# A hybrid mLSTM and window-attention decoder step on one core: all eight K tiles of the output product as seven products of sums of blocks

## The chip, the core and the metric

The kernel runs on one core of one Trainium2 chip. The metric is the device time of one execution in microseconds (us). TensorE is called PE here, its weight loads PEld, VectorE DVE, ScalarE ACT, GpSimd POOL and SyncE SP; SP issues most of the DMAs and is a queue in order like the others.

## The reference, cut to what matters

One layer of a decoder, for 1024 prompt rows and 32 sample rows (8 sequences of 4), all in float32 with D_MODEL = 1024:

```python
(mq, mk, mv, mi, mf, mo, mz, aq, ak, av, az, gm, ga) = split_in(h @ w_in)
y_m, C, n, m = mlstm_branch(mq, mk, mv, mi, mf, mo, mz, C0, n0, m0, b_i, b_f, g_mn)
...
y_a = o.astype(x.dtype) * jax.nn.silu(az)
u = jax.nn.sigmoid(gm) * (y_m @ w_mo) + jax.nn.sigmoid(ga) * (y_a @ w_ao)
x = x + gate * (u @ w_o)
```

followed by a final RMSNorm of x. The last product, u @ w_o (1024 + 32 rows, 1024 x 1024 weights), is the output product that this change is about. The gate is multiplied into the weights beforehand.

## The kernel before

A float32 product on PE is made of three products of rounded parts: each operand is split into a high part (a copy by ACT that rounds) and a low part (a subtract on DVE, the operand less its high part), and PE adds high by high, high by low and low by high. Such a split of a tile of 128x512 is one ACT copy and one DVE subtract; the names are wh_/wl_ for weights, h and l at the end of other names.

The program runs through these stages on PE: inputs and conditions; the "jobs" of queries and heads; eighteen "pairs" (class Pair, run by block_products), which form the gates and the remaining input products; the products of the attention output (att_products); eight jobs of w_m_out (mem_out, tile names g_w_mo, 288 matmuls of 384 or 288 columns); the output product in four blocks of 256 rows (class Rows; accumulators foX, foZ, foW, foY); and a short tail of norms and stores.

Pairs, attention output and part of the output product use the scheme of seven products for 2 x 2 blocks (Strassen in Winograd's form): four blocks of the one operand and four of the other become seven sums each, named 1 to 7, and seven products of half the K and half the columns take the place of eight. On the side of the weights the seven are b11, b21, b22, t1, t2, t3 and t4 (the table OPERANDS). [...]

Before the change the output product was mixed. K tiles 0 to 3 went through the seven products: two K tiles by three parts, six matmuls of 128x512 for each product, 42 for a block of 256 rows. K tiles 4 to 7 went plainly: 4 tiles by 3 parts by 4 accumulators, 48 matmuls. A block of rows had 90.

What sets the order of the work: PE's instructions run in the order in which the program writes them (in_order). In the middle part of the program DVE and ACT aren't tied to that order (V.on = S.on = False from L1935): the scheduler of the language orders them by its own estimates, and a multiplication written under not_before may not move ahead of the instruction written before it. From the row stage on (L2214) they are in written order again. Once built, every engine takes its instructions strictly in its own order. The class Side runs side work as generators in streams beside the pairs: each yield gives the time after which the next step may be written. Three of them matter here:

- stream "g", out_weights (L1964): started at pair 5, product 6. It loads w_out in tiles of 128x512 (wor), multiplies them by the gate (gb), forms the sums for K tiles 0 to 3 (wost, wos) and stores 22 tiles of float32 in DRAM (woD).
- the samples' heads, sample_head(h) (L1179): a chain of small operations on DVE, ACT and PE for the 32 sample rows. For h = 1 and h = 3 it ends with the tile sz being scaled on DVE (two small TENSOR_SCALAR), transposed on PE into sty (two matmuls at L280), and read by gs on DVE. fsden, fsv, fsr_w and fsr_y are the small steps of its reciprocal roots.
- the last four pairs are head_gate (names phead_gate): hg1z, hg, gts and zt are their evacuations on DVE, wr_mo, wr_mz and ws their raw weights and sums, and bx, bz, bw, by their accumulators.

In the stage of the w_m_out jobs the 22 stored tiles were loaded back into raw tiles and split there: high parts on ACT, low parts (wo_..l) on DVE and POOL in turns. A job of w_m_out has three pieces of columns (384, 384, 288); each piece is evacuated by a SCALAR_TENSOR_TENSOR (tgw_mo) and an add into u (u_h, u_l), on POOL for the last two jobs. The weights of a job, wr_w_mo, are split into wh_w_mo and wl_w_mo ahead of it; the third matmul of a job is the first that reads wl_w_mo.

Of the kernel before, what the change touches and what calls it, by code (L numbers as in the profile page):

```python
# [20 lines left out]
D = 1024  # L21
# [152 lines left out]
def body(tc, a):  # L174
    nc = tc.nc
    with ExitStack() as ctx:
# [1429 lines left out]
        u = lambda k, c0, n: ut[k // 4][:, k % 4, c0:c0 + n]  # L1606
# [36 lines left out]
        class AttPair:  # L1643
# [28 lines left out]
            def samples_end(self):  # L1672
                o = pb([128, 64], "smpo")
                mm(o, self.sums, cst[:, C_S64:C_S64 + 64], start=True, stop=True)
                us = ut[self.i // 2][:, 2 * self.i % 4:2 * self.i % 4 + 2, SEQ:T]
                V.scalar_tensor_tensor(us, self.ts, 1.0, o.rearrange("p (c s) -> p c s", c=2), op0=ALU.add, op1=ALU.mult)
# [287 lines left out]
        def out_weights():  # L1964
# [5 lines left out]
            def keep(name, k, t):  # L1970
                woD[name, k] = dp.tile([128, 512], F32, name=f"woD{name}{k}")
                store(woD[name, k], t)

            def load(ks):
                raws = {}
                for k in ks:
                    for f in range(2):
                        raws[k, f] = ht([128, 512], f"wor{k}{f}")
                        dma(raws[k, f], a["w_out"][k * 128:(k + 1) * 128, HALF[f]])
                return raws  # L1980

            def summed(n, k, x, y, op):
                t = ht([128, 512], f"wos{n}{k}")
                V.tensor_tensor(t, x, y, op=op)
                keep(n, k, t)
                return t

            lots = (4,), (5,), (6,), (7,), (0, 2), (1, 3)
            ahead = [load(lots[0])]
            yield 5.0, ""  # L1990
            for i, ks in enumerate(lots):
                raws = ahead.pop()
                if i + 1 < len(lots):
                    ahead.append(load(lots[i + 1]))
                yield 3.0, ""
                for (k, f), t in raws.items():
                    with not_before(V):
                        V.tensor_tensor(t, t, gb[f], op=ALU.mult)
                    if len(ks) == 1:
                        keep(f"p{f}", k, t)  # L2000
                    elif (k, f) != (ks[0], 1):
                        keep(("b11", "", "b21", "b22")[2 * (k // 2) + f], ks[0], t)
                    yield 2.4, ""
                if len(ks) == 2:
                    k = ks[0]
                    b11, b12, b21, b22 = raws.values()
                    t3 = summed("t3", k, b22, b12, ALU.subtract)
                    yield 2.4, ""
                    summed("t1", k, b12, b11, ALU.subtract)
                    yield 2.4, ""  # L2010
                    t2 = summed("t2", k, b11, t3, ALU.add)
                    yield 2.4, ""
                    summed("t4", k, b21, t2, ALU.subtract)
                    yield 2.4, ""

# [39 lines left out]
        class Rows:  # L2055


            def __init__(self, i):
                self.i, self.w, self.g = i, {}, {}
                self.x = [[t[:, :, (2 * i + c) * 128:(2 * i + c + 1) * 128] for t in ut] for c in range(2)]  # L2060

            def split(self, n, src, home, o):
                if home not in self.g:
                    self.g[home] = [ht([128, 4, 128], f"u{t}{home}", F32R) if home == "E" else
                                    granule(f"u{self.i}{t}{home}", t, 4, F32R) for t in ("wh", "wl")]
                hi, lo = (t[:, o:o + src.shape[1]] for t in self.g[home])
                S.copy(hi, src)
                V.tensor_tensor(lo, src, hi.bitcast(F32), op=ALU.subtract)
                self.w[n] = hi, lo

            def start(self, *ns):
                (a1, p1), (a2, p2) = self.x
                for n in ns:
                    if n == 1:
                        self.s = blocks_of_rows[self.i - 1].x[1][0][:, 2:4] if self.i else at["qpad"].rearrange("p b k g t -> p (b k g t)").rearrange("p (c e) -> p c e", e=128)
                        self.split(1, a1[:, 0:2], "A", 0)
                        V.tensor_tensor(self.s, a2[:, 0:2], a2[:, 2:4], op=ALU.add)
                    elif n == 5:
                        self.split(5, self.s, "A", 2)
                        V.tensor_tensor(a2[:, 0:2], a1[:, 0:2], a2[:, 0:2], op=ALU.subtract)  # L2080
                        V.tensor_tensor(a1[:, 0:2], self.s, a1[:, 0:2], op=ALU.subtract)
                    elif n == 2:
                        self.split(2, a1[:, 2:4], "B", 0)
                        V.tensor_tensor(a1[:, 2:4], a1[:, 2:4], a1[:, 0:2], op=ALU.subtract)
                    else:
                        self.split(n, *{6: (a1[:, 0:2], "B", 2), "p1": (p1, "C", 0), "p2": (p2, "D", 0), 7: (a2[:, 0:2], "E", 2),
                                        3: (a1[:, 2:4], "E", 0), 4: (a2[:, 2:4], "F", 0)}[n])

            def product(self, n, o, first, c0=0, w=512):
                hi, lo = self.w[n]  # L2090
                for k in range(2):
# [3 lines left out]
                    mm(o, lo[:, k], bh, start=False, stop=(k == 1), more=not first)  # L2095

            def plain(self, c, th, o, ks=range(4), c0=0, w=512):
                hi, lo = self.w[f"p{c + 1}"]
                for k in ks:
                    bh, bl = (t[:, c0:c0 + w] for t in plain[4 + k, th])  # L2100
                    mm(o, hi[:, k], bh, start=False, stop=False, more=True)
                    mm(o, hi[:, k], bl, start=False, stop=False, more=True)
                    mm(o, lo[:, k], bh, start=False, stop=(k == ks[-1]), more=True)

        blocks_of_rows = [Rows(i) for i in range(4)]
        wo, plain = {n: {} for n in ("b11", "b21", "b22", "t1", "t2", "t3", "t4")}, {}
        parts = [(n, k) for k in range(2) for n in ("b11", "t1", "b21", "t2", "b22", "t3", "t4")] + [(f"p{f}", k) for k in range(4, KT) for f in range(2)]
        side.finish("g")
        for d in range(KT):
            if d == KT - 1:  # L2110
                blocks_of_rows[0].start(1, 5, 2, 6)
            mem_out(d, ymx, u)
            for j in range(min(22, d * 26 // KT), min(22, (d + 1) * 26 // KT)):
                n, k = parts[j]
                raw = raw_tile(f"wo{n}{k}").rearrange("p k n -> p (k n)")
                dma(raw, woD[n, k], True)
                hi = ht([128, 512], f"wo_{n}h", F32R)
                lo = ht([128, 512], f"wo_{n}l", F32R) if j < 15 else granule(f"wo_{n}l", "wr", 9, F32R).rearrange("p k n -> p (k n)")
                S.copy(hi, raw)
                (G if j % 2 else V).tensor_tensor(lo, raw, hi.bitcast(F32), op=ALU.subtract)  # L2120
                if n[0] == "p":
                    plain[k, int(n[1])] = hi, lo
                else:
                    wo[n][k] = hi, lo

# [14 lines left out]
        def add_row(xb, c, src, kept=None):  # L2140
            if kept is not None:
                V.tensor_tensor(kept, kept, src, op=ALU.add)
            V.tensor_tensor(xb[:, c], xb[:, c], src if kept is None else kept, op=ALU.add)
# [25 lines left out]
        def sample_rows():  # L2169
# [14 lines left out]
            for f in range(2):  # L2184
# [4 lines left out]
                sums.append(raw_tile("fo8s").rearrange("p k n -> p (k n)")[:NS])  # L2189
# [16 lines left out]
        def copied(src, name, pool=None, c=slice(0, 512), new=None):  # L2206
            t = ht([128, 512], name) if pool is None else pool([128, 512], name)[:, :c.stop - c.start]
            if new:
                mm(t, new.w[1][0][:, 0], wo["b11"][0][0][:, c], start=True, stop=True)
# [7 lines left out]
        blocks_of_rows[0].start("p1")  # L2217
        xb = ss = None
        for i, r in enumerate(blocks_of_rows):
            nxt = blocks_of_rows[i + 1] if i < 3 else None  # L2220
# [3 lines left out]
            X, Z = pg([128, 512], "foX"), pa([128, 512], "foZ")  # L2224
            r.product(1, X, True)
            W = copied(X, "foW", pg, new=r if i == 0 else None)
            if i:
                add_row(before[0][1], lo, Y[0])
            r.product(5, Z, True)
            p5 = copied(Z, "fop5")  # L2230
            r.start("p2", 7, 3)
# [8 lines left out]
            if not nxt:  # L2240
                for c in range(2):
                    rows_out(4 + c, before[0][c], rs[:, c:c + 1])
            r.product(2, X, False)
            r.plain(0, 0, X)
# [139 lines left out]
```

## Time and profile before

| | us |
|---|---|
| median of 3 runs | 830.18 |
| range of the runs | 829.81 to 830.42 |
| the profiled execution | 829.68 |
| its span | 827.9 |
| PE busy | 810.2 |
| DVE busy | 590.5 |
| ACT busy | 419.0 |
| POOL busy | 67.2 |

A row of the page's group view names the line, the engine, the operation, the tile written and the tiles read, the shape, and then the busy time, the mean of one and the idle time ahead of it. In the timeline a row begins with start and duration in us, and ends, where the engine idled before it, with the idle time and what released it. A matmul's duration includes its drain, so that its pitch, from one start to the next, is shorter than its duration. A row of the windows view gives a stretch, its length, and for each engine its busy time and (x) its instructions, then the clock that PE was granted as a share of full speed, the DMA engines' busy share and GB/s.

### The profile page before, as it was taken

Reading aid. Unit: us, or ns where it says so; the run is one execution under the profiler, and the core shown is the slowest. Engines: PE = TensorE matmul, PEld = TensorE weight load, DVE = VectorE, ACT = ScalarE, POOL = GpSimd, SP = SyncE. Lnnn points to the kernel's source line nnn. Section 1 sums busy time; section 2 is a strip of 40 time slices with the busy share of each in tenths; the row PEclk is TensorE's granted clock in tenths of the full one; section 3 lists DMA queues with packets and bytes.
Section 4 is the critical chain, followed back from the end, with each engine's and each line's share of the span. In section 5 each row is a group of like instructions: output and inputs, shape, how many; then the busy total and the mean of one; then the engine's idle time right before and its main releaser. Section 6 shows DMA issues by size and latency. Waiting matters only on the chain.

```text
span 827.9 us, 15032 instructions
## 1 busy us (share of the span) xinstructions
PE 810.2 (98%) x5129; PEld 670.4 (81%) x5129; DVE 590.5 (71%) x1479; ACT 419.0 (51%) x1030; POOL 67.2 (8%) x128
## 2 busy tenths in 40 slices
PE   6999999999999999999999999999999999999996
PEld 3779897888787888888888878888888789987775
DVE  4899886746646456475667886897669988864776
ACT  5664365556455564545455454544446654344343
POOL 0120000000000001000001010000002104250000
PEclk9999999999999999999999999999999999999998
DMA  9994757456535415538867444454446685643532
GB/s 335 377 341 137 225 183 233 140 163 195 176 124 187 140 65 168 177 124 270 262 209 255 159 136 137 139 180 160 136 127 202 217 298 172 202 153 116 202 109 108
DMA packets 106689, 153.95 MB, mean 186 GB/s; under 512 B 20449, under 2 KB 54369, under 8 KB 106581
## 3 DMA queue, kind: packets, MB, share of 16 engines
q1 hardware_dynamic: 100964, 142.25, 52.4%
q10 hardware_dynamic: 4176, 6.56, 2.2%
q0 software_dynamic: 1472, 4.20, 1.3%
q8 instruction: 40, 0.66, 0.3%
q14 instruction: 37, 0.30, 0.1%
HBM read 109.22 MB, written 44.75 MB: 186 GB/s over the span
## 4 chain that ended last, share of the span: by engine, by line
PE 87%; DMA 4%; issue 4%; DVE 2%; ACT 1%; SPq 1%; DVEq 0%; POOLq 0%; POOL 0%
PE bx L275 10%; PE bw L275 10%; PE by L275 10%; PE g_aq L275 6%; PE g_w_mo L275 6%; PE bz L275 5%; PE foW L275 3%; PE foX L275 3%; PE foY L275 2%; PE smp L275 2%; PE g_mq L275 2%; PE foZ L275 2%; PE sc L275 2%; PE oT L275 2%; PE pt L280 2%
## 5 line engine op out<-in xcount | busy, mean ns | idle before, releaser
L220 ACT ACTIVATE p<-p,nmx 128x256 f32<-128x256 f32 (+1 forms) x64 | 31.0, 486 | 18.7 <-DVE nmx L220 18.4
L275 PE MATMUL g_aq<-h_h,wh_aq 128*128 128x384 f32 (+1 forms) x96 | 32.3, 336 | 0.0
L275 PE MATMUL g_aq<-h_h,wl_aq 128*128 128x384 f32 (+1 forms) x96 | 30.9, 322 | 0.0
L275 PE MATMUL g_aq<-h_l,wh_aq 128*128 128x384 f32 (+1 forms) x96 | 30.9, 322 | 0.0
L275 PE MATMUL g_w_mo<-ym_h,wh_w_mo 128*128 128x384 f32 (+1 forms) x96 | 30.8, 321 | 0.0
L275 PE MATMUL g_w_mo<-ym_l,wh_w_mo 128*128 128x384 f32 (+1 forms) x96 | 30.8, 321 | 0.0
L275 PE MATMUL g_w_mo<-ym_l,wl_w_mo 128*128 128x384 f32 (+1 forms) x96 | 30.8, 321 | 0.0
L220 DVE CUSTOM_DVE_ANT_0 p<-sc,cst,sink 128x256 f32<-128x256 f32 (+1 forms) x64 | 26.1, 463 | 5.3 <-PE sc L275 5.2
L261 POOL DMA_DIRECT2D oD<-uqv x16 | 8.8, 552 | 183.7 <-ACT uqv L220 163.8
L275 PEld LDWEIGHTS g_aq<-h_h,wh_aq 128*128 128x128 f32 x96 | 18.0, 188 | 2.6 <-issue 1.5
L275 PEld LDWEIGHTS g_w_mo<-ym_l,wh_w_mo 128*128 128x128 f32 x96 | 18.0, 188 | 0.0
L275 PE MATMUL sc<-ukv,uqv 64*128 64x256 f32 (+1 forms) x128 | 18.0, 390 | 0.1
L275 PEld LDWEIGHTS g_aq<-h_l,wh_aq 128*128 128x128 f32 x96 | 18.1, 188 | 0.0
L275 PEld LDWEIGHTS g_w_mo<-ym_h,wh_w_mo 128*128 128x128 f32 x96 | 18.0, 188 | 0.0
L275 PEld LDWEIGHTS g_aq<-h_h,wl_aq 128*128 128x128 f32 x96 | 18.0, 188 | 0.0
L275 PEld LDWEIGHTS g_w_mo<-ym_l,wl_w_mo 128*128 128x128 f32 x96 | 18.0, 188 | 0.0
L220 DVE COPY p<-pt 128x512 f32<-128x512 f32 (+1 forms) x16 | 10.5, 655 | 10.3 <-PE pt L280 10.3
L220 DVE TENSOR_TENSOR et<-et,S 128x384 f32<-128x384 f32 (+1 forms) x12 | 6.1, 509 | 16.1 <-PE S L275 13.4
L275 PE MATMUL g_mq<-h_h,wh_mq 128*128 128x384 f32 (+1 forms) x48 | 16.8, 350 | 0.3 <-ACT mk L220 0.3
L220 ACT ACTIVATE sq<-rows_h 128x512 f32<-128x512 f32 (+2 forms) x14 | 8.2, 583 | 17.7 <-issue 12.0
L280 PE MATMUL pt<-cst,p 128*128 128x128 f32 x120 | 16.4, 277 | 0.5 <-DVE mx L220 0.5
L220 ACT ACTIVATE p<-p,den 128x256 f32<-128x256 f32 (+1 forms) x32 | 14.2, 490 | 3.7 <-DVE den L220 3.7
(2073 smaller groups left out, 2840.6 us busy)
## 6 DMA issues: line engine op xcount, KB each, us to landing
x<-xT SPq DMA_DIRECT2D x16, 256.0 KB
early_h<-w_ada SPq DMA_DIRECT2D x8, 512.0 KB
adar_ga<-w_ada SPq DMA_DIRECT2D x16, 256.0 KB
wr_ga<-w SPq DMA_DIRECT2D x16, 256.0 KB
wr_gm<-w SPq DMA_DIRECT2D x16, 256.0 KB
taD<-gt SPq DMA_DIRECT2D x16, 256.0 KB
tmD<-gt SPq DMA_DIRECT2D x16, 256.0 KB
wor<-w_out SPq DMA_DIRECT2D x16, 256.0 KB
```

What stands on the lines that cost most here:

```text
L220: ins = f(*args, **kw)
L261: ins = (eng or nc.sync).dma_start(out, in_)
L275: in_order(nc.tensor.matmul(out, lhsT, rhs, start=start, stop=stop, skip_group_check=more))
L280: in_order(nc.tensor.transpose(out, in_, idn))
```

## The change

The output product takes all eight K tiles through the seven products: four K tiles by three parts, 12 matmuls for each product, 84 for a block of rows. The plain part and its tables go. To pair the K tiles, u is laid out so that tiles k and k + 2 (of 0 to 3 and of 4 to 7) are the two blocks. Each sum on the side of the rows is now 128x512 instead of 128x256, and is started one product ahead (row_start).

out_weights now makes four lots of four tiles (KA = 0, 1, 4, 5): 16 multiplications by the gate, 16 sums, and 28 splits into high and low parts (an ACT copy and a DVE subtract each, tiles wosh and wosl), and 56 stores in DRAM; before it made 16 multiplications, 8 sums and 22 stores. The stage of w_m_out loads the 56 tiles straight to where the products read them (weights_out); nothing is split there for w_out, POOL has no part in it any more, and the adds into u are all on DVE.

```diff
-        def mem_out(d, y, u):
+        def mem_out(d, y, u, mid):
...
-                (G if d > 5 else V).tensor_tensor(us, us, t, op=ALU.add)
-            job(("w_mo", d), ev, None, *y, 4)
+                V.tensor_tensor(us, us, t, op=ALU.add)
+            job(("w_mo", d), ev, mid, *y, 4)
...
-        u = lambda k, c0, n: ut[k // 4][:, k % 4, c0:c0 + n]
+        u = lambda k, c0, n: ut[k // 2 % 2][:, k // 4 * 2 + k % 2, c0:c0 + n]
...
+            def keep(n, k, t):
+                parts = [ht([128, 512], f"wos{x}", F32R) for x in "hl"]
+                S.copy(parts[0], t)
+                V.tensor_tensor(parts[1], t, parts[0].bitcast(F32), op=ALU.subtract)
+                woD[n, k] = [dp.tile([128, 512], F32, name=f"woD{n}{k}{x}") for x in "hl"]
+                for d, x in zip(woD[n, k], parts):
+                    due.append((side.now + 4.0, d, x.bitcast(F32)))
+
+            for k in KA:
+                raws = []
+                for kk in (k, k + 2):
                     for f in range(2):
+                        raws.append(ht([128, 512], f"wor{k}{f}"))
+                        dma(raws[-1], a["w_out"][kk * 128:(kk + 1) * 128, HALF[f]])
+                yield 10.0, ""
+                for j, t in enumerate(raws):
                     with not_before(V):
+                        V.tensor_tensor(t, t, gb[j % 2], op=ALU.mult)
                     yield 2.4, ""
+                b11, b12, b21, b22 = raws
+                t3 = ht([128, 512], f"wot3{k}")
+                V.tensor_tensor(t3, b22, b12, op=ALU.subtract)
+                keep("b22", k, b22)
+                yield WLAG, ""
+                V.tensor_tensor(b12, b12, b11, op=ALU.subtract)
+                keep("t1", k, b12)
+                yield WLAG, ""
...
+        KA, WLAG = (0, 1, 4, 5), 4.0
...
             def product(self, n, o, first, c0=0, w=512):
                 hi, lo = self.w[n]
-                for k in range(2):
+                for k in range(4):
...
-            def plain(self, c, th, o, ks=range(4), c0=0, w=512):
...
+        def weights_out(n):
+            for _ in range(n):
+                n, k = wo_parts.pop(0)
+                aside = len(wo_parts) < 8
+                hi = ht([128, 512], f"wo_{n}h", F32R)
+                lo = granule(f"wo_{n}l", "wr", 9, F32R).rearrange("p k n -> p (k n)") if aside else ht([128, 512], f"wo_{n}l", F32R)
+                for t, d in zip((hi, lo), woD[n, k]):
+                    dma(t.bitcast(F32), d, True)
+                wo[n].append((hi, lo))
...
-                blocks_of_rows[0].start(1, 5, 2, 6)
-            mem_out(d, ymx, u)
-            for j in range(min(22, d * 26 // KT), min(22, (d + 1) * 26 // KT)):
-                n, k = parts[j]
-                raw = raw_tile(f"wo{n}{k}").rearrange("p k n -> p (k n)")
-                dma(raw, woD[n, k], True)
...
-                S.copy(hi, raw)
-                (G if j % 2 else V).tensor_tensor(lo, raw, hi.bitcast(F32), op=ALU.subtract)
...
+                row_start()
+            mem_out(d, ymx, u, row_start if d == KT - 1 else None)
+            if d < 6:
+                weights_out((4, 4, 4, 3, 3, 3)[d])
+        weights_out(len(wo_parts))
```

PE's order is the same up to the first matmul into foX, the start of the row stage; behind that there are 24 matmuls of 128x512 less. What moves ahead of it is DVE's order, at two places.

The first is the end of sample_head(3), among the head_gate pairs. In PE's order of the changed kernel the two transposes sty stand right behind the product into by (operand t3) and ahead of the next pair's first product into bx; this piece reads the same before, but for the numbers in the names:

```order
L275 MATMUL by<-t3h_1685,wh_phead_gate_7__6972 128x512
L275 MATMUL by<-t3l_1686,wh_phead_gate_7__6972 128x512
L275 MATMUL by<-t3h_1685,wl_phead_gate_7__6973 128x512
L280 MATMUL sty_7075<-cst,sz 128x104 x2
L275 MATMUL bx<-h_h_378,wh_phead_gate_1__6995 128x512
L275 MATMUL bx<-h_l_379,wh_phead_gate_1__6995 128x512
L275 MATMUL bx<-h_h_378,wl_phead_gate_1__6996 128x512
```

On DVE, before the change, sz was scaled (the TENSOR_SCALAR) nine rows ahead of hg1z, which reads that product by:

```order
L220 SCALAR_TENSOR_TENSOR fsr_y<-fsr_w,fsr_y 32x2
L220 TENSOR_SCALAR sz<-sz,fsden,fsr_y 32x128 x2
L220 TENSOR_TENSOR ws_6883<-wr_mz_0_6765,wr_mz_1_6767 128x512
L220 TENSOR_TENSOR wl_phead_gate_3__6888<-wr_mo_1_6527,wh_phead_gate_3__6887 128x512
L220 TENSOR_TENSOR wl_phead_gate_4__6914<-wr_mz_1_6531,wh_phead_gate_4__6913 128x512
L220 SCALAR_TENSOR_TENSOR gts<-gts,smpo 128x32
L220 TENSOR_TENSOR wr_mz_0_6765<-wr_mo_0_6761,wr_mz_0_6765 128x512
L220 SCALAR_TENSOR_TENSOR gts<-gts 128x32
L220 TENSOR_TENSOR wr_mo_0_6761<-ws_6883,wr_mo_0_6761 128x512
L220 TENSOR_TENSOR gts<-gts,gs 128x32
L220 TENSOR_TENSOR hg1z<-p_6811,by 128x512
L220 TENSOR_SCALAR gs<-sty_6908,vec 128x32 x2
```

On DVE, in the changed kernel:

```order
L220 TENSOR_TENSOR hg1z<-p_6959,by 128x512
L220 TENSOR_TENSOR fsr_w<-fsr_w,fsv 32x2
L220 TENSOR_TENSOR wl_phead_gate_5__7104<-ws_7048,wh_phead_gate_5__7103 128x512
L220 SCALAR_TENSOR_TENSOR fsr_y<-fsr_w,fsr_y 32x2
L220 SCALAR_TENSOR_TENSOR hg_7068<-hg_7068,hg1z 128x512
L220 TENSOR_TENSOR fsr_w<-fsr_y 32x2
L220 TENSOR_TENSOR wosl<-wor_6491,wosh 128x512
L220 TENSOR_TENSOR fsr_w<-fsr_w,fsv 32x2
L220 TENSOR_TENSOR wor_6491<-wor_6491,wor_6487 128x512
L220 SCALAR_TENSOR_TENSOR fsr_y<-fsr_w,fsr_y 32x2
L220 TENSOR_SCALAR sz<-sz,fsden,fsr_y 32x128 x2
L220 TENSOR_TENSOR wosl<-wor_6491,wosh 128x512
```

There hg1z stands ahead of sz, with nine rows between them, four of them 128x512; two of the four are of the output weights' last lot (wosl, wor).

The second place is the stage of the w_m_out jobs. On DVE before the change, around the last piece (128x288) of a job, the next job's split wl_w_mo stands ahead of that piece's evacuation:

```order
L220 SCALAR_TENSOR_TENSOR tgw_mo_0_8442<-tgw_mo_0_8442,g_w_mo_8527 128x384
L220 SCALAR_TENSOR_TENSOR tgw_mo_1_8444<-tgw_mo_1_8444,g_w_mo_8542 128x384
L220 TENSOR_TENSOR wl_w_mo_0_8524<-wr_w_mo_0_8452,wh_w_mo_0_8523 128x512
L220 SCALAR_TENSOR_TENSOR tgw_mo_2_8446<-tgw_mo_2_8446,g_w_mo_8557 128x288
L220 TENSOR_TENSOR wo_p0l<-wop_8499,wo_p0h 128x512
L220 TENSOR_TENSOR u0wlA<-u_h_7571,u0whA 128x256
```

In the changed kernel the split stands behind that evacuation; here at two jobs, and ahead of the last job it reads the same:

```order
L220 TENSOR_TENSOR u_h_7755<-u_h_7755,tgw_mo_1_8466 128x384
L220 SCALAR_TENSOR_TENSOR tgw_mo_2_8468<-tgw_mo_2_8468,g_w_mo_8575 128x288
L220 TENSOR_TENSOR wl_w_mo_0_8540<-wr_w_mo_0_8474,wh_w_mo_0_8539 128x512
L220 TENSOR_TENSOR u_h_7755<-u_h_7755,tgw_mo_2_8468 128x288
L220 SCALAR_TENSOR_TENSOR tgw_mo_0_8533<-tgw_mo_0_8533,g_w_mo_8614 128x384
L220 SCALAR_TENSOR_TENSOR tgw_mo_1_8535<-tgw_mo_1_8535,g_w_mo_8629 128x384
L220 TENSOR_TENSOR u_h_7755<-u_h_7755,tgw_mo_0_8533 128x384
L220 TENSOR_TENSOR u_h_7755<-u_h_7755,tgw_mo_1_8535 128x384
L220 SCALAR_TENSOR_TENSOR tgw_mo_2_8537<-tgw_mo_2_8537,g_w_mo_8644 128x288
L220 TENSOR_TENSOR wl_w_mo_0_8609<-wr_w_mo_0_8543,wh_w_mo_0_8608 128x512
L220 TENSOR_TENSOR u_h_7755<-u_h_7755,tgw_mo_2_8537 128x288
```

On PE of the changed kernel, the end of one job and the start of the next, whose third matmul is the first to read the low part wl_w_mo_0_8540; this order is as before:

```order
L275 MATMUL g_w_mo_8575<-ym_l_7543,wl_w_mo_0_8471 128x288
L275 MATMUL g_w_mo_8614<-ym_l_7543,wh_w_mo_0_8539 128x384
L275 MATMUL g_w_mo_8614<-ym_h_7544,wh_w_mo_0_8539 128x384
L275 MATMUL g_w_mo_8614<-ym_l_7543,wl_w_mo_0_8540 128x384
L275 MATMUL g_w_mo_8614<-ym_l_7543,wh_w_mo_0_8539 128x384
L275 MATMUL g_w_mo_8614<-ym_h_7544,wh_w_mo_0_8539 128x384
```

So the split moved from ahead of the wait for the last piece of the job before to behind it, for three of the eight jobs.

More of the change, by code (lines that the diff above doesn't have):

```diff
@@ L1982, in summed @@
[L1982 to L1996, printed above, removed]
-                    with not_before(V):
[L1998 to L2002, printed above, removed]
-                    yield 2.4, ""
[L2004 to L2014, printed above, removed]
@@ new lines, in start @@
+            def start(self, n):
+                (a11, a12), (a21, a22) = self.x
+                if n == 1:
+                    self.split(1, a11)
+                elif n == 5:
+                    self.s = blocks_of_rows[self.i - 1].x[1][0] if self.i else ht([128, 4, 128], "us")
+                    V.tensor_tensor(self.s, a21, a22, op=ALU.add)
+                    self.split(5, self.s)
+                    V.tensor_tensor(a21, a11, a21, op=ALU.subtract)
+                    V.tensor_tensor(a11, self.s, a11, op=ALU.subtract)
+                elif n == 2:
+                    self.split(2, a12)
+                    V.tensor_tensor(a12, a12, a11, op=ALU.subtract)
+                else:
+                    self.split(n, {6: a11, 7: a21, 3: a12, 4: a22}[n])
@@ L2208, in copied @@
             if new:
-                mm(t, new.w[1][0][:, 0], wo["b11"][0][0][:, c], start=True, stop=True)
+                mm(t, new[0][:, 0], wo["b11"][0][0][:, c], start=True, stop=True)
             S.copy(t, src[:, c])
@@ L2239, in body @@
                 rs = norm_rows(before[1], 2 if nxt else 3, 2)
[L2240 to L2244, printed above, removed]
+            for x in xb:
+                add_row(x, hi, Z)
+            row_start()
             r.product(6, W, False)
             parts = ((0, 512),) if nxt else ((0, 256), (256, 256))
-            Y = [copied(W, f"foY{c0}", pb if c0 else pa, slice(c0, c0 + n), r if c0 or i == 0 else None) for c0, n in parts]
+            Y = [copied(W, f"foY{c0}", pb if c0 else pa, slice(c0, c0 + n), r.w[6] if c0 or i == 0 else None) for c0, n in parts]
             aside(1, 2)
+            for c in range(2) if i else ():
+                rows_out(2 * i - 2 + c, before[0][c], rs[:, c:c + 1])
+            row_start()
+            r.product(2, X, False)
             add_row(xb[0], lo, X)
-            r.start(4)
-            if nxt:
-                nxt.start(1)
-            else:
-                square(xb[0][:, lo], ss[:, 0:1])
-            r.plain(1, 1, Z, range(2))
-            y7 = ht([128, 512], "foy7")
+            aside(1, 2)
+            square(xb[0][:, lo], ss[:, 0:1])
             def seventh():
```

116 lines of the change are left out of this document (39 added, 77 removed).

## Prediction

> **What bounds the kernel now.** I read the page's busy times first, then the chain of waits by engine, then PE's waits over the whole span, and last the windows of the stages that the change touches.
>
> ```profile
> PE 810.2 (98%) x5129; PEld 670.4 (81%) x5129; DVE 590.5 (71%) x1479; ACT 419.0 (51%) x1030; POOL 67.2 (8%) x128
> PE 87%; DMA 4%; issue 4%; DVE 2%; ACT 1%; SPq 1%; DVEq 0%; POOLq 0%; POOL 0%
> PE xc L275 <- ACT xsq L220: 6.5, 1, 6.5
> ...
> PE smp L275 <- DMA wr_gm<-w: 0.5, 2, 0.3
> ...
> PE aw L275 <- ACT aw L220: 0.2, 1, 0.2
> 536.00:580.00 44.00, 44.00 (x271) 36.12 (x270) 37.92 (x91) 20.23 (x44) 3.17 (x13) 1.00 0.51 167
> 687.00:733.00 46.00, 46.00 (x290) 45.96 (x289) 39.79 (x67) 14.82 (x27) 16.79 (x12) 1.00 0.54 174
> 733.00:828.00 95.00, 87.74 (x421) 69.69 (x420) 62.19 (x134) 39.70 (x99) 6.08 (x5) 0.98 0.43 147
> ```
>
> PE is busy 98% of the span and 87% of the chain that ended last is PE. Of its waits only the first, 6.5 us at the start, is large; the list ends at 0.2. So every matmul that goes is worth its pitch, and every wait that comes is paid in full: there is no slack on PE in which a new one could hide. DVE has 37.92 of 44 us in the stretch of the head_gate pairs (fourth column), and 39.79 of 46 in the w_m_out jobs: it keeps up, with six us to spare in each.
>
> **What goes: 24 matmuls.** The row stage has 4 x 90 = 360 products before and 4 x 84 = 336 now, all of 128x512 or its halves. The pitch is read from the chain of waits in that stage, where runs of 18 stand back to back (its first row is where the stage starts):
>
> ```profile
> 733.25 1.38 PE foX L275 x6
> ...
> 746.00 4.08 PE foW L275 x18
> ...
> 758.11 4.08 PE foX L275 x18
> ```
>
> 4.08 / 18 = 0.2267 us, so 24 of them are 5.44 us. PE had no wait in this stage, so the whole of it is gained if the weights are there. The additions into the rows, the copies and the norms of the stage are a few DVE and ACT operations fewer; they weren't on the path. The splits of the weights on DVE and POOL in the stage before go too, and that gains nothing: PE is at 46.00 of 46.
>
> **What comes at the end of sample_head(3).** PE takes its instructions in order, and the two transposes sty stand behind the product into by and ahead of the next product into bx. They need sz.
>
> ```profile
> 577.73 0.39 PE L275 MATMUL by<-t3h,wl_phead_gate__6816 128*128 128x512 f32 x1
> 577.97 0.34 PE L280 MATMUL sty<-cst,sz 104*128 104x104 f32 x2
> 570.97 0.15 DVE L220 SCALAR_TENSOR_TENSOR fsr_y<-fsr_w,fsr_y 32x2 f32<-32x2 f32 x1
> 571.15 0.59 DVE L220 TENSOR_SCALAR sz<-sz,fsden,fsr_y 32x128 f32<-32x128 f32 x2
> 578.16 0.69 DVE L220 TENSOR_TENSOR hg1z<-p,by 128x512 f32<-128x512 f32 x1 [1.43 <-PE by L275]
> 578.77 0.40 DVE L220 TENSOR_SCALAR gs<-sty,vec 128x32 f32<-128x32 f32 x2
> 579.09 0.68 DVE L220 TENSOR_TENSOR wl_phead_gate__6931<-ws,wh_phead_gate__6930 128x512 fp32r<-128x512 f32 x1
> 579.69 0.69 DVE L220 SCALAR_TENSOR_TENSOR hg<-hg,hg1z 128x512 f32<-128x512 f32 x1
> ```
>
> Before, sz was ready at 571.15 + 0.59 = 571.74, 6.2 us ahead of its reader at 577.97. hg1z waits for the last matmul of by (released at 578.16), the matmul just ahead of sty on PE. In the changed DVE order hg1z stands ahead of sz. So sz can't be written before by is done, and PE must idle from the end of by until DVE has gone through what lies between. That is a bound from below that needs no lateness of DVE: from hg1z at 578.16, four operations of 128x512 behind it and itself, at the pitch of 0.60 (579.09 to 579.69), are 3.0; five small ones at 0.18 (570.97 to 571.15) are 0.9; the pair sz itself 0.6: 578.16 + 4.5 = 582.7, against 577.97. The wait is at least 4.7 us.
>
> The bound from above is what DVE has to do in all. From the first addition of sU into Cs of the second to last head, which PE releases, to sz DVE has 27 operations more than before: 24 of 128x512 (14 of the last lot of output weights, ten that now stand ahead of sz) and three small, 24 x 0.605 + 3 x 0.18 = 15.1. Between those points it idled only twice:
>
> ```profile
> 536.63 0.55 DVE L220 TENSOR_TENSOR Cs<-Cs,sU 128x387 f32<-128x387 f32 x1
> 540.32 0.69 DVE L220 TENSOR_TENSOR ztz<-p,bw 128x512 f32<-128x512 f32 x1 [1.13 <-PE bw L275]
> 562.67 0.69 DVE L220 TENSOR_TENSOR ztz<-p,bw 128x512 f32<-128x512 f32 x1 [0.97 <-PE bw L275]
> ```
>
> 15.1 less 2.1 of idle and less 6.2 of slack leaves 6.8. Both ends are counts of the same queue, the one from where by frees it and the other from where sU does; I take 6.0, nearer the upper, since DVE should come to hg1z a little late: it has the whole lot ahead of it. All of PE's work is queued behind the waiting transposes; the splits of the next three products stand ahead of sz on DVE, so no second wait follows at once. The three earlier lots meet pairs with no such reader in their way; DVE has 21 operations of 128x512 more in all there (45 for 24) and ACT 21 of the 28 copies. Bounds: 0, since those stretches have DVE time to spare, and 1.5, three lots at the 0.5 that PE's list has for smp in the pairs; I take 0.5.
>
> **What comes in the w_m_out jobs.** For the last three jobs the split wl_w_mo stands behind the last piece's evacuation of the job before.
>
> ```profile
> 727.35 0.33 PE L275 MATMUL g_w_mo<-ym_l,wh_w_mo 128*128 128x384 f32 x1
> 727.52 0.34 PE L275 MATMUL g_w_mo<-ym_h,wh_w_mo 128*128 128x384 f32 x1
> 727.70 0.34 PE L275 MATMUL g_w_mo<-ym_l,wl_w_mo 128*128 128x384 f32 x1
> 726.44 0.69 DVE L220 TENSOR_TENSOR wl_w_mo<-wr_w_mo,wh_w_mo 128x512 fp32r<-128x512 f32 x1
> 727.55 0.46 DVE L220 SCALAR_TENSOR_TENSOR tgw_mo<-tgw_mo,g_w_mo 128x288 f32<-128x288 f32 x1 [0.42 <-PE g_w_mo L275]
> 727.92 0.68 DVE L220 TENSOR_TENSOR wo_p0l<-wop,wo_p0h 128x512 fp32r<-128x512 f32 x1
> ```
>
> This is the boundary of the last job. The evacuation starts when PE ends the piece, 727.55; the operation behind it starts at 727.92 and takes 0.68, to 728.60. That operation will be the split; PE's third matmul, which reads it, is due at 727.70. 0.90 us each, 2.7 for three. It would be nothing if ym_l,wl weren't the third; the rows say that it is. Between 2.4 and 3.0 with what a semaphore takes.
>
> **The weights' way.** 56 tiles of 128x512 floats are 14.7 MB where 22 tiles (5.8 MB) were loaded: 8.9 MB more. All but the first products can have theirs later: seven products of 12 x 0.2267 = 2.72 us follow one another, so the last operand is due 16 us into the stage. The 46 us of jobs carried 46 x 174 = 8.0 MB; 16.9 MB in 46 + 16 = 62 us are 273 GB/s, a share of 0.54 x 273 / 174 = 0.85. It fits, and I cost it at nothing; the cover is those 62 us, and only a rate below the 273 costs time.
>
> **The clock of PE.** The trace shows it once PE ends, its last matmul starting at 820.46:
>
> ```profile
> 820.46 0.28 PE L275 MATMUL foY<-wo_p0h,u3wlD 128*128 128x256 f32 x1
> 823.25:823.50 0.25, 0.00 (x0) 0.00 (x0) 0.25 (x1) 0.25 (x1) 0.00 (x0) 1.00 0.00 0
> 823.75:824.00 0.25, 0.00 (x0) 0.00 (x0) 0.07 (x1) 0.04 (x1) 0.00 (x0) 0.50 0.00 0
> 7.34 4.96 PE L275 MATMUL xs<-xsq,one 128*32 128x512 f32 x16
> 13.96 3.65 PE L275 MATMUL xs<-xsq,one 128*32 128x512 f32 x16
> ```
>
> It falls to 0.50 some 2.9 us after PE went idle. The wait for sz is longer than that, so PE should start again at half speed. What that costs the start of the program shows: the same sixteen matmuls took 4.96 after the idle 6.5 us and 3.65 later, 1.3 more. Bounds: 0, if the wait ends sooner than the gate acts, and 2.4, half of the 4.96 us at full length; I take 1.3. The waits of 0.9 are too short. [...]
>
> **The sum.** -5.44 + 6.0 + 0.5 + 2.7 + 1.3 = +5.1 us. Against the profiled execution, 829.68, that is 834.8; the median of the runs is 0.5 higher, and on that scale I predict 835.2. From the lower bounds: -5.44 + 4.7 + 0 + 2.4 + 0 = +1.7; from the upper: -5.44 + 6.8 + 1.5 + 3.0 + 2.4 = +8.3.
>
> **Rivals.** **(a)** PE doesn't wait for sz, since DVE runs ahead: then only the jobs' waits and the pairs' 0.5 stand against the gain, -5.44 + 2.7 + 0.5 = -2.2, 828.0, faster. Six us of slack speak for it, the place of hg1z against it: what would have to be wrong is that the transposes wait for a DVE operation behind one that waits for by. It decides where the wait falls below 0.5. 0.09. (b) The wait comes, but the clock stays up: 830.2 - 5.44 + 6.0 + 0.5 + 2.7 = 834.0; the trace has no wait of 3 us or more amid work that could tell. 0.25. (c) The loads starve the products: SP's queue is in order, and the last 20 or so tiles (t3, b22 and t4, 5.2 MB) wait for buffers that the evacuations of the last jobs free, just ahead of 733. t4 is due 16 us on: at 350 GB/s (the page's second slice moved 377) 5.2 MB take 15 us, at 325 or less the products wait. For it speaks that no stage before asked for so much while DVE and PE run, against it that the queue reached its rate at the start:
>
> ```profile
> GB/s 335 377 341 137 225 183 233 140 163 195 176 124 187 140 65 168 177 124 270 262 209 255 159 136 137 139 180 160 136 127 202 217 298 172 202 153 116 202 109 108
> ```
>
> At 250 it is 21 us and PE waits 5: 840. 0.12. (d) The change is a clean gain, all new work hidden: 830.2 - 5.4 = 824.7. 0.03. (e) The upper bounds at both places and in the earlier lots: 830.2 + 8.3 = 838.5. 0.08.
>
> **How the numbers follow.** The forecast, with clock and both waits, has 0.43. What a measurement of this kernel can tell from no change is 0.2%, 1.7 us: 828.5 to 831.8. Of (a) a fifth ends as the same, so faster has 0.07 + 0.03 = 0.10. The lower bounds at every place at once end at 831.9, just at the limit; for that corner of (b) I give 0.09, so the same has 0.11 and slower 0.79. The range reaches from 830.0 to 840.5: it leaves out (a), (d) and most of (c). The forecast's own range is 832.5 to 838.
>
> **What would show it.** In the changed profile: PE's waits list sty with 4.7 to 6.8 us, released by DVE sz, and g_w_mo three times with about 0.9, released by DVE wl_w_mo; the granted clock below 1.00 in the window behind sty; the row stage with 336 matmuls at the same pitch and no waits on DMA, its length down by 5.4. I am wrong if PE's list has no sty, if foX to foY wait for DMAs wo_t4 or wo_b22, or if the end moves without any of these.

## The result, and the profile after

| | before | after |
|---|---|---|
| median of 4 runs, us | 829.99 | 835.40 |
| range of the runs, us | 829.35 to 830.42 | 833.81 to 835.85 |
| profiled execution, us | 829.68 | 833.81 |
| its span, us | 827.9 | 832.0 |

The ratio is 1.0062, with a 95% interval of 1.0045 to 1.0080: the kernel is slower by 5.4 us, beyond what the measurement could confuse with no change. The profiled execution is the quickest of the four, 4.1 us above that of before.

PE's waits over the whole span of the changed kernel, in us: total, times, longest.

```profile
PE xc L275 <- ACT xsq L220: 6.8, 1, 6.8
PE sty L280 <- DVE sz L220: 4.2, 1, 4.2
PE g_w_mo L275 <- DVE wl_w_mo L220: 2.4, 3, 0.8
...
PE foY L275 <- DVE rows_h L220: 0.4, 1, 0.4
PE smp L275 <- ACT gts L220: 0.4, 1, 0.4
PE ty L280 <- ACT smps L220: 0.4, 1, 0.4
```

The waits at the two places that the order of DVE had shown are there, with the releasers that it named. No product of the row stage waits for a DMA.

The timeline of PE and then of DVE around the first of them, the wait for sz (start, duration, and at the end the idle time before the row):

```profile
577.04 0.39 PE L275 MATMUL by<-t3h,wl_phead_gate__6973 128*128 128x512 f32 x1
581.58 0.60 PE L280 MATMUL sty<-cst,sz 104*128 104x104 f32 x2 [4.15 <-DVE sz L220]
581.88 0.78 PE L275 MATMUL bx<-h_h,wh_phead_gate__6995 128*128 128x512 f32 x1
...
583.30 0.63 PE L275 MATMUL bx<-h_h,wh_phead_gate__6995 128*128 128x512 f32 x1
583.73 0.63 PE L275 MATMUL bx<-h_l,wh_phead_gate__6995 128*128 128x512 f32 x1
```

```profile
576.89 0.67 DVE L220 TENSOR_TENSOR wr_mo<-ws,wr_mo 128x512 f32<-128x512 f32 x1
577.49 0.14 DVE L220 TENSOR_TENSOR fsr_w<-fsr_y 32x2 f32<-32x2 f32 x1
577.56 0.67 DVE L220 TENSOR_TENSOR hg1z<-p,by 128x512 f32<-128x512 f32 x1
578.16 0.14 DVE L220 TENSOR_TENSOR fsr_w<-fsr_w,fsv 32x2 f32<-32x2 f32 x1
578.23 0.67 DVE L220 TENSOR_TENSOR wl_phead_gate__7104<-ws,wh_phead_gate__7103 128x512 fp32r<-128x512 f32 x1
...
581.10 0.59 DVE L220 TENSOR_SCALAR sz<-sz,fsden,fsr_y 32x128 f32<-32x128 f32 x2
```

The row of hg1z bears no idle time: DVE was busy up to it and reached it just as by was done (577.04 + 0.39). So the two limits that the prediction counted, the place behind hg1z and the length of the queue, meet here, and the timeline alone can't tell which of the two makes PE wait. Behind the wait the matmuls stand 0.43 us apart (583.30 to 583.73) instead of 0.23. The windows view around it shows the clock (the number before the last two of a row):

```profile
580.00:581.50 1.50, 0.00 (x0) 1.00 0.74 273
581.50:582.50 1.00, 0.92 (x4) 0.53 0.99 307
582.50:583.50 1.00, 1.00 (x4) 0.50 0.83 270
583.50:584.50 1.00, 1.00 (x4) 0.50 1.09 262
584.50:585.50 1.00, 1.00 (x5) 0.77 0.82 285
```

0.53 in a stretch of 1 us that ends at half speed puts the fall at 581.56, and 0.77 puts the rise at 584.96: half speed for 3.4 us.

The second place, at the start of the sixth job, PE and then DVE:

```profile
722.44 0.45 PE L275 MATMUL g_w_mo<-ym_l,wl_w_mo 128*128 128x384 f32 x1 [0.80 <-DVE wl_w_mo L220]
```

```profile
721.33 0.45 DVE L220 SCALAR_TENSOR_TENSOR tgw_mo<-tgw_mo,g_w_mo 128x288 f32<-128x288 f32 x1
721.70 0.68 DVE L220 TENSOR_TENSOR wl_w_mo<-wr_w_mo,wh_w_mo 128x512 fp32r<-128x512 f32 x1
```

Where the 4.2 us between the two spans of the profiled executions lie, from the start times of the same matmuls on PE:

| stretch of PE | before, us | after, us | difference |
|---|---|---|---|
| start to the first sty | 516.16 | 515.47 | -0.7 |
| to the sty of sample_head(3) | 61.80 | 66.10 | +4.3 |
| to the first product of the attention output | 66.67 | 68.41 | +1.7 |
| to the first w_m_out matmul | 42.51 | 42.42 | -0.1 |
| to the first foX | 45.95 | 49.20 | +3.3 |
| to the last matmul | 87.36 | 82.63 | -4.7 |
| to the end of the span | 7.41 | 7.81 | +0.4 |

The first row holds a gain that I had not forecast. Matching the matmuls one by one, the changed kernel is 0.7 us behind by 383 us, mostly from two DMA waits near 55 and 92 us, where the two kernels are still the same. Then it gains 1.7 us at two gaps around 384 us, where before the samples' matmuls waited for a weight's DMA; the time lost is longer than the idle time in the rows, since a row's time runs to the end of the drain: of the 0.64 us from 384.41 to 385.05 the two matmuls ahead have 0.41 and the idle time 0.24:

```profile
383.35 0.80 PE L275 MATMUL smp<-wr_ga,c 128*32 128x128 f32 x4
384.41 0.41 PE L275 MATMUL smp<-wr_gm,c 128*32 128x128 f32 x2 [0.26 <-DMA wr_gm<-w]
385.05 0.30 PE L275 MATMUL smp<-wr_gm,c 128*32 128x128 f32 x1 [0.24 <-DMA wr_gm<-w]
```

In the changed kernel the same matmuls follow one another from 384.07 without a wait: SP issued that weight's load at 373.73, and before the change at 378.27. Before, SP had stood still for 4.4 us at another load (qw) that waited for a store (yhD) to land; in the changed kernel it doesn't wait there. What took that wait away isn't shown; another assignment of buffers would do it. A further 0.8 us are gained at two places near 406 and 416 us, and 1.0 us is lost again near 484 and 488 us, at the waits smp and ty of the list above.

### The profile page after: what moved, and what is told of

Its sections match the earlier page's. It is cut to its first block, busy times and chain, and to the rows that moved or that the text cites. A ratio compares the mean times of both kernels' runs of the same rounds, so it can differ in the third digit from the quotient of the medians.

```text
span 832.0 us, 15086 instructions
## 1 busy us (share of the span) xinstructions
PE 805.9 (97%) x5105; PEld 666.3 (80%) x5105; DVE 604.6 (73%) x1503; ACT 417.9 (50%) x1019; POOL 47.5 (6%) x111
## 4 chain that ended last, share of the span: by engine, by line
PE 80%; DVE 11%; DMA 3%; issue 3%; ACT 2%; SPq 1%; DVEq 0%; ACTq 0%
PE bx L275 11%; PE bw L275 10%; PE by L275 10%; PE g_w_mo L275 6%; PE bz L275 5%; PE g_mq L275 3%; PE g_aq L275 3%; PE foX L275 2%; PE sc L275 2%; PE oT L275 2%; PE smp L275 2%; PE pt L280 2%; PE foW L275 2%; PE n L275 2%; PE g_mv L275 1%
## 5 line engine op out<-in xcount | busy, mean ns | idle before, releaser
L220 DVE SCALAR_TENSOR_TENSOR tgw_mo<-tgw_mo,g_w_mo 128x384 f32<-128x384 f32 (+1 forms) x24 | 12.5, 520 | 19.7 <-PE g_w_mo L275 18.2
L220 DVE TENSOR_TENSOR wosl<-wor,wosh 128x512 fp32r<-128x512 f32 x24 | 16.5, 686 | 3.7 <-ACT wosh L220 3.0
L220 ACT CAST wh_w_mo<-wr_w_mo 128x512 fp32r<-128x512 f32 x8 | 4.9, 622 | 26.1 <-DMA wr_w_mo<-w_mo 17.1
L220 ACT CAST wosh<-wor 128x512 fp32r<-128x512 f32 x24 | 14.9, 621 | 4.8 <-DVE wor L220 2.0
```

The costliest lines, as they stand in the source:

```text
L220: ins = f(*args, **kw)
```

## The experiments

All were run beside the kernel before on the same chip; ratios are to that. Those with the splits in written order are compared with the first of them. The kernel before had a median of 829.33 us beside the first four runs, 829.43 beside the next four and 830.26 beside the last, so ratios compare better than medians.

**The splits wl_w_mo in written order.** DVE's instructions from the w_m_out jobs on keep the order of the program, in which a job's split is written ahead of the pieces of the job before.

```diff
         side.finish("g")
+        V.on = True
         for d in range(KT):
```

> Theory: PE's waits are additive, each from a DVE operation that stands too late in DVE's order. With the splits wl_w_mo ahead of the pieces of the job before, the three waits of 0.8 us go and nothing else moves: 835.4 - 2.4 = 833.0, the wait for sz and the half clock behind it stay. Rival (DVE or the loads are the bound in the w_m_out jobs): the waits come back under another name, 835.4.

Measured: 831.45 us, ratio 1.0029 (1.0017 to 1.0041), where the change had 1.0062. PE's list has no wait for wl_w_mo any more, the stretch of the jobs is back at 45.95 us, and the wait for sz is the same 4.2. The theory holds: the ratio falls by 0.0033, which is 2.7 us, for 2.4 us of listed waits.

**PE kept busy in the wait.** 24 dummy matmuls ahead of the transposes sty; they add work whose results aren't used. From 581.88 to 584.99 in the changed kernel seven matmuls behind sty took some 0.2 us more each than at full clock; by that estimate a clock that stays up saves 1.4 us, 834.0.

```diff
+            if h == NH - 1:
+                then = side.now, side.products
+                warm(24)
+                side.now, side.products = then
             ty = pb([128, 2, 128], f"sty{h}")
```

> 24 dummy matmuls of 128x128 stand ahead of the transposes sty; their results are not used. [...] Rival (the half clock costs nothing, since DVE is late anyway behind the wait): 835.4.

Measured: 833.62 us, ratio 1.0057 (1.0044 to 1.0069). In its trace the clock stays at 1.00 to the tail, and from the sty of sample_head(3) to the attention output PE takes 66.64 us, as before the change (66.67), where the changed kernel took 68.41. So the half clock costs 1.7 us of PE's time in the profiled execution. The timing by itself doesn't confirm it: the ratios differ by 0.0005, less than their intervals. One reason is in the trace. The dummies became 48 matmuls and kept PE from 576.33 to 581.68, 5.35 us instead of the 4.1 that I had reckoned (24 at 0.17). sz started at 580.17, and sty follows the start of sz by 0.48 in the changed kernel, so that the dummies held sty back by 1.0 us of their own.

**The transposes later on PE.** The yield ahead of sty raised, so that it is written some 6 us later.

```diff
-            yield 4.0, "b"
+            yield 10.0, "b"
             ty = pb([128, 2, 128], f"sty{h}")
```

> The transposes sty stand two and a half products later in PE's order. Theory: the wait for sz (4.2) and the clock's cost (1.4 to 3) go: 828.2 to 829.8; the three waits of the w_m_out jobs stay. Rival (DVE's backlog is the bound, and the wait only moves to the next reader): a wait of 3 us or more elsewhere in the pairs, 833 or more.

Measured: 833.24 us, ratio 1.0052 (1.0038 to 1.0066): the rival. PE's list no longer has sty, and has two others, smp near 528 us and bx at 535 us (the row of g_w_mo is that of the jobs, as expected):

```profile
PE bx L275 <- DVE zt L220: 2.4, 1, 2.4
PE g_w_mo L275 <- DVE wl_w_mo L220: 2.4, 3, 0.8
PE smp L275 <- DVE sz L220: 1.2, 1, 1.2
```

The edit also moves the end of sample_head(1) and with it side work, so that the lots stand elsewhere; but 3.6 us of waits on DVE come back at other readers, ahead of sty and not behind it as the rival has it, and the clock falls to half behind the second, at 535.49.

**Both edits.**

> Both edits. Theory: the effects add up and only the gain of the row stage is left, less 0.4 of foY: 825.8 to 827.4, faster than the kernel before. Rival (one bound behind the other): no better than the better of the two alone, 829 to 830.

Measured: 831.3 us, ratio 1.0021 (1.0012 to 1.0031), no better than the splits alone within the intervals. Its trace has the two new waits, 3.6 us again, and never falls to half clock amid work; but that execution, 829.5 us, is the quickest of ten. Six of the others were granted a mean clock of 0.995 or 0.996, which no execution of the kernel before has, and took 831.4 us on average. The effects don't add up to the gain of the row stage: DVE is late in the pairs, and moving one reader isn't enough.

**Only the order of hg1z and sz.** On top of the splits in written order, hg1z may not stand ahead of sz on DVE.

```diff
+                sum_ = V.tensor_tensor(z, src[0], src[1], op=ALU.add)
+                if name == "hg1":
+                    no_sync(getattr(sum_, "ins", sum_), [getattr(i, "ins", i) for i in szs])
```

> On top of the splits wl_w_mo in written order (831.4): on DVE hg1z may not stand ahead of sz any more, everything else as the scheduler places it. Order theory (only hg1z ahead of sz makes PE wait): no wait for sz, clock at 1.00: 831.4 - 4.2 - 1.7 = 825.5. Load theory (DVE reached hg1z just as its product ended, because of the last lot of output weights ahead of it): sz comes only the two operations sooner that now stand behind it, 1.3 us; PE waits 2.9, 830.1, or 828.4 if that is too short for the clock to fall.

Measured: 828.96 us, ratio 0.9989 (0.9980 to 0.9998). PE still waits for sz:

```profile
PE sty L280 <- DVE sz L220: 2.1, 1, 2.1
```

Of the 4.2 us the order makes 2.1; the other 2.1 stay with sz ahead of hg1z and are the queue. That lies between the two theories and nearer to the load: I had 2.9 for it, with hg1z and hg behind sz, and the scheduler put two operations of the lot behind it as well, so that part of the first 2.1 is queue too.

**The output weights two pairs sooner.** The same work, the last lot through before the end of sample_head(3); on top of the splits in written order.

```diff
-        OUT_WEIGHTS = 5
+        OUT_WEIGHTS = 3
```

> On top of the splits wl_w_mo in written order (831.4): the stream of the output weights starts two pairs sooner, so that its last lot is through before the end of sample_head(3); the amount of work is the same. Load theory: no wait for sz and no fall of the clock, 831.4 - 4.2 - 1.7 = 825.5. Rival (DVE is full in all pairs, wherever the lots stand, as the run with the later transposes hints): waits of 2 us or more on DVE at other readers in the pairs, 828 to 831.

Measured: 826.67 us, ratio 0.9960 (0.9946 to 0.9974): faster than both kernels. No wait for sz, no fall of the clock amid work. With the lot gone, the scheduler also puts sz ahead of hg1z again (572.14 and 579.16 us), so this run takes away both causes of the wait, the order and the queue; only the run above holds them apart. The windows of the stretch from 536 to 580 us show why, in DVE's column (the third with an x), in the changed kernel and in this one; before the change it was 37.92:

```profile
536.00:580.00 44.00, 41.43 (x258) 33.61 (x256) 43.55 (x99) 23.98 (x51) 5.76 (x13) 1.00 0.73 241
```

```profile
536.00:580.00 44.00, 44.00 (x272) 36.10 (x271) 37.93 (x91) 20.37 (x45) 3.19 (x13) 1.00 0.54 169
```

43.55 of 44 us: DVE was full there, and PE's 44 had become 41.43. The rival isn't wholly wrong: one wait came at another place, 1.0 us of bx for ACT gt, which is most of the 1.2 us by which the time is above what was expected.

**The last lot's subtracts on POOL.** On top of the splits in written order.

```diff
-                V.tensor_tensor(parts[1], t, parts[0].bitcast(F32), op=ALU.subtract)
+                (G if k == 5 else V).tensor_tensor(parts[1], t, parts[0].bitcast(F32), op=ALU.subtract)
```

> On top of the splits wl_w_mo in written order (831.4): the seven low-part subtracts of the last lot run on POOL instead of DVE. Load theory: DVE has 7 x 0.605 = 4.2 us less ahead of sz, which is about the wait: no wait, clock at 1.00, 825.5. Rival (a subtract on POOL makes DVE's operations beside it longer, 1.0 to 1.8 us instead of 0.68 in the trace of before): the relief is eaten up, a wait of 2 to 4 us stays, 829 to 831.

Measured: 828.07 us, ratio 0.9985 (0.9976 to 0.9995), between the two. A subtract took 1.66 us on POOL instead of 0.67, and operations on DVE beside it grew:

```profile
L220 POOL TENSOR_TENSOR wosl<-wor,wosh 128x512 fp32r<-128x512 f32 x6 | 9.9, 1656 | 26.0 <-ACT wosh L220 26.0
```

```profile
568.66 1.80 DVE L220 SCALAR_TENSOR_TENSOR zt<-zt,ztz 128x512 f32<-128x512 f32 x1
```

A wait of 1.7 us stays at sty, with sz ahead of hg1z here as well. The clock didn't fall behind it in this trace; one of the ten executions, with a mean clock of 0.995, is likely to have had a fall.

**The lots closer together.** On top of the splits in written order.

```diff
-        KA, WLAG = (0, 1, 4, 5), 4.0
+        KA, WLAG = (0, 1, 4, 5), 2.4
```

> On top of the splits wl_w_mo in written order (831.4): the lots follow one another faster (2.4 us of the writing clock between splits instead of 4.0), so the last lot is through before the end of sample_head(3) and DVE has more to do per us before. Load theory: as with the earlier start, 825.5. Rival: DVE's denser work makes PE wait earlier, 828 to 831; the run with the earlier start should then be the better one.

Measured: 830.71 us, ratio 1.0013 (1.0003 to 1.0024): the rival. The wait for sz is gone, and others are there instead: 2.1 us in two pieces at ty for DVE et, the longer of 1.5 us ending at 444.08, with a fall of the clock at 446.30. The same work in less time makes DVE late sooner. Another 2.1 at foW in the row stage isn't due to the lots: DVE stood there for 1.9 us at an addition that waited for a load of x, ahead of the split that foW reads, and the second trace of the kernel with sz ahead of hg1z, whose lots aren't moved, has 1.5 us at the same place.

**The earlier stream by itself.** OUT_WEIGHTS 3 and nothing else.

> The stream of the output weights starts two pairs sooner, and nothing else is changed: the splits wl_w_mo stand where the change left them. If the two causes are independent, the three waits of 0.8 us in the w_m_out jobs are back and the wait for sz is gone: 826.7 + 2.4 to 3.0 = 829.1 to 829.7. If the earlier stream also helped the jobs, 826.7 to 828.

Measured: 830.01 us, ratio 1.0000 (0.9990 to 1.0010), with wl_w_mo back at 2.4 us and no sty. Within the intervals the two causes are independent: 1.0062 falls to 1.0029 by the one edit, to 1.0000 by the other, and to 0.9960 by both.

**The clock in a second trace.** The changed kernel and the one with sz ahead of hg1z were profiled once more, one execution each (834.18 and 830.39 us).

> The changed kernel once more, for its clock. In the runs so far the clock rose at the start and fell behind the wait at a distance that is a whole multiple of 3.413 us (167 of them), and stayed at half for one more. [...] Rival (the clock falls a fixed time after PE goes idle, some 2.9 us as in the tail): the fall comes 2.9 us after the last matmul of by, 580.4 in this run's scale, in all runs.

> The kernel with sz ahead of hg1z once more: a wait of 2.1 us. [...]

Measured: by the trace's record of the clock, the distance from its rise at the start to its first fall was 570.03 us in both traces of the changed kernel, and 570.03 and 566.61 in the two of the other. The last differs from the rest by 3.42, and in the first trace the clock then stood at half for 3.413 us; the distances are 167, 167, 167 and 166 times that. It fell 4.1 and 4.6 us after the matmuls of by ended in the changed kernel, and 3.0 and 1.9 in the two of the other. The rows of the windows view for the last, whose wait began at 577.39 and ended at 579.53, put the fall at 579.33 and the rise at 582.74:

```profile
579.00:579.50 0.50, 0.00 (x0) 0.83 0.45 146
579.50:580.00 0.50, 0.47 (x3) 0.50 0.12 37
582.00:583.00 1.00, 1.00 (x4) 0.63 0.70 260
```

A fixed delay after the idle start is out; in the tails of the thirteen traces, too, the fall comes between 2.1 and 5.2 us after the last matmul (2.9 before the change, 2.8 after). The rise comes 4.4 to 6.5 us after PE's first matmul in the four traces, at no fixed time either. Every fall seen amid work lasted the same 3.41 us. What sets its moment isn't shown.

The same wait doesn't always cost the clock. A wait of 2.4 us for zt stands in the run with the later transposes and in the one with both edits; its row and the clock behind it, first in the one and then in the other:

```profile
534.97 0.50 PE L275 MATMUL bx<-h_h,wh_pquery_gate__6417 128*128 128x512 f32 x1 [2.41 <-DVE zt L220]
535.49:538.90 3.41, 3.41 (x9) 2.64 (x9) 2.41 (x5) 0.00 (x0) 0.00 (x0) 0.50 0.87 241
```

```profile
536.61 0.50 PE L275 MATMUL bx<-h_h,wh_pquery_gate__6417 128*128 128x512 f32 x1 [2.41 <-DVE zt L220]
536.61:539.00 2.39, 2.39 (x10) 1.99 (x11) 2.31 (x5) 0.00 (x0) 0.00 (x0) 1.00 0.92 289
```

In the first the clock falls at 535.49, 0.52 us after PE has started again, and stands at half for 3.41 us. In the second it stays at 1.00. So the length of a wait alone doesn't decide it: the clock fell behind waits of 4.2, 2.4, 2.1 and 1.5 us, and not behind this one of 2.4 or the one of 1.7 in the run with the subtracts on POOL. What else does isn't shown.

So some waits of 2 us cost no clock. The timed executions fit that, though only their mean clock is known: with sz ahead of hg1z, six of the ten timed executions had a mean clock of 0.995 and took 829.2 us on average, the other four 0.997 or 0.998 and 828.1 us. All 54 executions of the kernel before that were timed beside the experiments have 0.997 to 0.999.

## Why the prediction was right, step by step

- **The gain of the row stage**: 5.44 forecast, 4.7 measured. The pitch and the count were right. The row stage got a new wait of foY for one of DVE's additions, 0.4 us in the list and 0.6 in the starts of the matmuls, which I had put at nothing; it is most of the difference.
- **The wait for sz**: 6.0 forecast, with bounds 4.7 and 6.8; the listed wait is 4.15, PE lost 4.3, below the lower bound. The step that was mis-sized is the small operations at 0.18. Behind a large one, four of the five cost 0.07 to 0.10 (578.16 to 578.23 is the first), so that hg1z to sz took 3.5 instead of 3.9. The upper bound has the same error: the seventeen operations on 32x2 in that count took 2.7 us of DVE's time before and 1.2 after, which takes 6.8 down to 5.3. So that DVE would come to hg1z late was wrong: it came just in time. The cause that I named, a place in the order and a full queue behind it, was right in both parts: the order makes about half of the wait, and with the last lot out of the way, and sz back ahead of hg1z, there is none.
- **The clock**: 1.3 forecast, 1.7 in the profiled execution, by the stretch behind sty and by the run with dummy matmuls. The tail's 2.9 us, which I took for a fixed delay after the idle start, is not one: behind the waits for sz the fall came 1.9 to 4.6 us after the last matmul. That waits of 0.9 are too short held, with the clock at 1.00 from 687 to 741.6, where the three of the jobs lie. A wait need not last those 2.9 us, though: the clock fell behind waits of 1.5, 2.1 and 2.4 us. It stood at half for 3.4 us, and half of that is the 1.7 measured; the row of the program's start that I chose gave 1.3.
- **The w_m_out jobs**: 2.7 forecast for three; 2.4 in the list, which counts from the end of a drain, 2.9 in the starts of the three matmuls (0.96 each) and 3.3 in the stretch; the last 0.4 I can't place. For the way from DVE to PE the prediction had only widened its bounds, without a row; it is 0.06 us here, from the end of the split (721.70 + 0.68) to the matmul at 722.44.
- **The earlier lots**: +0.5 forecast; 1.0 lost, and 2.5 gained, 1.7 of it at the weight's DMA. The gain was not foreseen, and that the lots cause it isn't shown.
- **The loads**: nothing forecast, and no product of the row stage waited for a DMA. The jobs ran with 288 GB/s over 49.2 us, and with the first 16 us of the row stage it is 276, where I had asked for 273.
- **The sum**: 835.2 forecast, 835.4 measured. The agreement to 0.2 us is luck. The forecast had the wait for sz 1.7 too long and the lots 2.0 too dear; against that stand 0.7 in the row stage, 0.6 in the jobs, 0.4 of the clock and 0.7 lost ahead of the lots, where the kernels are the same, all in the profiled execution, and the other three take longer than that one. It was at +4.1, and what separates it from the other three, 1.6 to 2.0 us, isn't settled: their mean clock is 0.993 and 0.994 instead of 0.995, and 0.002 of 834 us are 1.7 us, so that a second stretch of 3.4 us at half speed would fit, but they have no trace.

Of the rivals, that DVE runs ahead and PE doesn't wait was wrong for this kernel, and is what the earlier stream makes true. The clock didn't stay up in either trace. The starved loads didn't come.

## What to carry to other kernels

Where PE takes its work in order and is 98% busy, moving work to another engine is free only if that engine has time in the very stretch where it lands: DVE was busy for 71% of the span before and 73% after, and for 43.55 of 44 us in the stretch that mattered. Read the new order for two things, what an operation that PE waits for now stands behind, and whether that waits for PE itself; each such pair is a wait whose size can be counted in advance, here as 6.0 us for 4.3. And place moved work by the load, stretch by stretch, of the engine that gets it: here the same work two pairs sooner, and DVE in written order from the w_m_out jobs on, turned 0.6% slower into 0.4% faster.

## What the hardware showed that I had not expected

- Behind waits of 1.5 to 4.2 us the granted clock fell to half and stayed there for 3.41 us; with 0.43 us from matmul to matmul instead of 0.23 that is 1.7 us lost. The same wait of 2.4 us lost it in one run and not in another. From the clock's rise at the start to its fall it was 570.03 us in three of four traces of two kernels, and 566.61 in the fourth, 3.42 less.
- Between operations of 128x512, a DVE operation on 32x2 that doesn't depend on the one ahead took 0.07 to 0.10 us of the engine's time, and 0.18 in a chain of its own kind.
- A wait in the list of PE's waits is shorter than the time lost, by the drain of the matmul ahead: 0.80 listed, 0.96 us lost.
